# A hybrid attention layer on one core: projection pieces between the turns of attention of one k step in place of two

## The chip, the cores and the metric

One NeuronCore of a Trainium2 chip runs the whole layer in one launch. The metric is the device time of that launch in microseconds (us), as a median over runs. Five engines work side by side: TensorE (PE in the profile, with its weight loads as PEld), VectorE (DVE), ScalarE (ACT), GpSimd (POOL) and SyncE (SP), which here only issues DMAs.

## The reference: what is computed

One layer over 1024 positions of width 1024. The input is normalised and modulated by a condition, `u = LN(x) * (1 + scale) + shift`; one projection of `u` gives queries, keys, values and gates for 16 heads of 64 columns. Eight heads attend by softmax with a forget bias (FoX), eight by stick breaking. Each head's output is multiplied by `silu` of its gate branch, all are projected by `w_out`, and the gated residual is normalised again:

```python
u = (_layer_norm(x) * (1.0 + scale) + shift)
h = u @ w_in[layer]
fq, fk, fv, fg, ff, sq, sk, sv, sg = _split_columns(h)
# FoX:   s = q k^T * scale + (f_q - f_k), causal;  softmax(s) @ v
# stick: w = exp(log_sigmoid(z) + later), later = sum of log_sigmoid(-z) over later keys;  w @ v
y = jnp.concatenate([y_fox * silu(fg), y_sb * silu(sg)], axis=-1) @ w_out[layer]
x = _layer_norm(ALPHA * x + gate * y, ln_g, ln_b)
```

## The kernel before

Products keep float32 accuracy by splitting each operand in a high and a low part, so that one k step of a projection (128 of the 1024 input columns) is **three matmuls**: high by high, high by low, low by high. `u` stands transposed in SBUF as eight tiles `uh` and eight `ul`, one for each k step.

The heads go in eight pairs `p`; pairs 0 to 3 are stick breaking, 4 to 7 FoX. A **unit** `(p, h, i)` is one head of a pair and one block of 128 queries, and there are 128 units, counted `k` from 0. A unit takes two turns on TensorE:

- **scores turn** (`scores_turn`, L1060; `att_scores`, L447): the S matmuls (L459, L460) into the PSUM tile `S`, of which there is one (L71). Then ScalarE, VectorE and GpSimd make the weights from it. In pairs 0 to 3 ScalarE makes two sigmoids, `kp` (L481) and `be` (L483), VectorE runs the scan over `kp` (L488, L492), and GpSimd multiplies the two (L494). In pairs 4 to 7 VectorE adds the bias (L467), ScalarE exponentiates (L472), GpSimd scales (L475).
- **weights turn** (`weights_turn`, L1050; `att_transpose`, L499), two units later (`LAG`): the weights are transposed on TensorE, 128 columns at a time (L511, the tiles `T`), copied out by ScalarE (L513) and VectorE (L514), and for every second unit multiplied with the values (`att_pv`, L528).

Between these turns stands work of the next pairs, the **filler**: generators chained in one list (`fillers`, L997) that each do a piece and yield. `gen_m` (L321) makes a 128-column projection of queries, keys or gates: it fetches the weights (a DMA, then on GpSimd the high part, L126, and the low part, L127), yields, then runs two halves of 512 positions with eight k steps each (`m_step`, L296 to L298) and yields after every second step. `gen_v` and `v_tile` (L369, L348) make the values, 256 or 264 columns wide, for 128 positions at a time, with a yield in the middle and at the end; their weights come in four quarters, each read by two k steps. `gen_rest` finishes the projections of the start, `gen_last_g` (L983) the last gate, and loads the output weights as it goes. Three side tasks ride along, one call for each piece of their main chain (`beside`, L558): the adaLN gate, the forget bias and the splitting of `w_out`; their delays (`FLOG`, `FROW`, `GATE`, `SPACE`, L77 to L80) count pieces.

How many pieces a pair gets stands in `FILL` (L1007), 239 in all. The running sum `want` spreads them over two slots for each unit, nearly evenly, and `fill` (L1019) calls the chain until the count reaches the sum, so it rounds **up to whole pieces**. For the units of pairs 0 to 3 the loop (L1083) runs weights turn, scores turn, then both slots; from pair 4 on it runs scores turn, slot, weights turn, slot.

The order on TensorE is that in which the program is written. The other engines and SP's queue after the start are ordered by the scheduler of the framework. Weight buffers limit how early a fetch can run: two raw tiles (L115) and five high/low pairs in a ring (`RING`).

Of the kernel before, what the change touches and what calls it, by code (L numbers as in the profile page):

```python
# [27 lines left out]
def tile_hybrid_layer(  # L28
# [45 lines left out]
    RING = 5  # L74
    WARM = (4, 1, 1, 1, 1)
    NORM_ON = {6: nc.vector, 7: nc.vector}
    FLOG = 4  # L77
    FROW = 8
    GATE = 10
    SPACE = 5  # L80
    BEHIND = 1

    def after(*instructions):
# [226 lines left out]
    def make_g(p):  # L310
        sgt[p] = big("sg", 2, f"sg_{p}")
# [9 lines left out]
    def gen_m(p, m):  # L321
        tiles = fetch_m(p, m)
        yield
        (make_q, make_k, make_g)[m](p)
        for ch in ((1, 0) if m == 2 and p >= 4 else (0, 1)):
            acc = acc_tile(f"m_{p}_{m}_{ch}")
            for kt in range(NB):
                m_step(acc, tiles, kt, ch)
                if kt == NB - 1:
                    evac_m(p, m, ch, acc)  # L330
                if kt % 2 == 1:
                    yield


    fsb = cp.tile([P, 8, NB], F32, tag="fsb", name="fsb")
# [12 lines left out]
    def v_tile(g, t, acc, quarters):  # L348
        n = 264 if g == 1 else 256
        ts_ = slice(t * P, (t + 1) * P)  # L350
        for kt in range(NB):
            hi, lo = quarters[kt // 2]
            s = slice((kt % 2) * n, (kt % 2) * n + n)
            nc.tensor.matmul(acc[:, :n], u_hi[kt][:, ts_], hi[:, s], start=(kt == 0), stop=False)  # L354
            nc.tensor.matmul(acc[:, :n], u_lo[kt][:, ts_], hi[:, s], start=False, stop=False)  # L355
            nc.tensor.matmul(acc[:, :n], u_hi[kt][:, ts_], lo[:, s], start=False, stop=(kt == NB - 1))  # L356
            if kt == 3:
                yield
        for i in range(2):
            v4 = vt[2 * g + i].rearrange("p t (x c) -> p t x c", c=HD)  # L360
            a4 = acc[:, i * P:(i + 1) * P].rearrange("p (x c) -> p x c", c=HD)
            v_evacs.append(nc.scalar.copy(v4[:, t, 0::3, :], a4))
            v_evacs.append(nc.vector.tensor_tensor(v4[:, t, 1:3, :], a4, v4.bitcast(F32)[:, t, 0::3, :],
                                                   op=ALU.subtract))
        if g == 1:
            nc.vector.tensor_tensor(fsb[:, :, t], acc[:, 256:264], bf_sb, op=ALU.add)
        yield

    def gen_v(g, quarters=None, tiles=range(NB)):  # L369
        n = 264 if g == 1 else 256  # L370
        if quarters is None:
            quarters = []
            for h in range(4):
                src = w_vf[h] if g == 1 else w_v[g - (g > 1), h]
                quarters.append(fetch_w(f"v{g}_{h}", src, 2 * n))
        yield
        if g:
            make_v(g)
        for t in tiles:
            yield from v_tile(g, t, acc_tile(f"v_{g}_{t}"), quarters)  # L380

    def gen_forget():
# [23 lines left out]
        nc.tensor.matmul(fp, ones.to_broadcast([P, P]), pre, start=False, stop=True)  # L406
        fc = cp.tile([P, 64], F32, tag="fab", name="fc")
        nc.scalar.activation(fc, fp, AF.Copy, scale=-1.0)
        yield
        ft = t_tile("frow")[:64, :P]  # L410
        nc.tensor.transpose(ft, fc, ident)
# [349 lines left out]
    def gen_gate():  # L761
        b = att_tile("bg")
        nc.sync.dma_start(b, b_gate.to_broadcast([P, D]))
        for _ in range(GATE):
            yield
        parts = []
        for h in range(2):
            s = slice(h * 512, h * 512 + 512)
            hi, lo = (t[:, :512] for t in ring_w(f"gate_{h}"))
            nc.gpsimd.tensor_scalar(hi, gate[:, s], 1.0, 1.0, op0=ALU.mult, op1=ALU.mult)  # L770
            nc.gpsimd.tensor_tensor(lo, gate[:, s], hi.bitcast(F32), op=ALU.subtract)
            parts.append((hi, lo))
            for _ in range(2):
                yield
        for h in range(2):
            s = slice(h * 512, h * 512 + 512)
            gp = t_tile(f"gate_{h}")

            for i, part in enumerate(parts[h]):
                nc.tensor.matmul(gp, half.to_broadcast([P, P]), part, start=(i == 0), stop=(i == 1))  # L780
            nc.vector.scalar_tensor_tensor(gate[:, s], b[:, s], 0.5, gp, op0=ALU.mult, op1=ALU.add)
            yield

    def late_round(kb):
# [56 lines left out]
    def gen_rest():  # L841
        accs = {n: acc_tile(f"st_{n}b") for n in (3, 4)}
        order_of = {3: (3, 4, 5, 6, 7, 0, 1, 2), 4: range(NB)}
        for n in (3, 4):
            for j, kb in enumerate(order_of[n]):
                start_steps((n,), accs, kb, 512, 1024, ends=(j == 0, j == NB - 1))
                if j == NB - 1:
                    evac_m(*START[n], 1, accs[n])
                if j % 2:
                    yield  # L850

    bf_sb = cp.tile([P, 8], F32, tag="bf", name="bf_sb")
    nc.sync.dma_start(bf_sb, b_f.to_broadcast([P, 8]))
# [129 lines left out]
    def gen_last_g(p):  # L983
        tiles = fetch_m(p, 2)
        yield
        make_g(p)
        accs = {ch: acc_tile(f"m_{p}_2_{ch}") for ch in (1, 0)}
        for n in range(NB):
            for kt, ch in ([(0, 1 - n), (1, 1 - n)] if n < 2 else [(n, 1), (n, 0)]):
                m_step(accs[ch], tiles, kt, ch)  # L990
            if n == NB - 1:
                for ch in (1, 0):
                    evac_m(p, 2, ch, accs[ch])
            load_wo(n)
            yield

    fillers = chain([  # L997
# [6 lines left out]
                      gen_m(7, 0), gen_m(7, 1)]), gen_split_out()),  # L1004
        gen_last_g(7),
    ])
    FILL = (26, 36, 34, 34, 36, 36, 29, 8)  # L1007
    LEAD = 2
    LAG = 2
    W0 = 100.0  # L1010
# [35 lines left out]
    ready = []  # L1046
    LAST = 16 * (NPAIR - 1)
    tail = chain([gen_out_first(6), gen_out_last(6)] + [gen_out(t) for t in OUT_ORDER[1:]])
    fill(2)
    def weights_turn(k):  # L1050
        if LAG <= k < len(units) + LAG:
            u = units[k - LAG]
# [112 lines left out]
```

## Time and profile before

| | |
|---|---|
| median of 3 runs | 685.25 us (684.95, 685.25, 1349.6) |
| profiled execution, its own time | 685.27 us |
| its span, first to last instruction | 683.2 us |
| time around the span | 2.1 us |
| mean granted TensorE clock | 0.998 of full speed |

The span falls into a start (to about 81 us, where the projections of the first pair stand), the eight pairs of attention with the filler between their turns (81 to 564 us), and the rest of the last pair with the output projection. The busy time of TensorE has modelled ends: neighbouring matmuls overlap in it, so what a matmul costs is read from start to start in the timeline (a 128x512 matmul is listed with some 0.39 us, and the next starts 0.23 us behind it). `[0.38 <-POOL be L494]` behind a row of the timeline tells how long the engine had been idle and who ended it.

### The profile page before, as it was taken

The numbers are of one execution on the slowest core, as the hardware profiler recorded it, in microseconds if no ns is written. First come the engines' busy times: TensorE is split into PE (matmuls) and PEld (weight loads), VectorE is DVE, ScalarE is ACT, GpSimd is POOL, SyncE is SP. The second block draws the span as 40 slices with busy tenths as digits, with TensorE's granted clock in tenths as the row PEclk, the third lists the DMA queues.
The fourth block names the chain that finished last, engine by engine and source line by source line (L and its number), as shares of the span: only waits on it lengthen the run. The fifth ranks groups of instructions, "written<-read, shape, count | busy, mean of one in ns | idle before, by whom it ended". The sixth has DMA issues, their size and how long they took to land.

```text
span 683.2 us, 11185 instructions
## 1 busy us (share of the span) xinstructions
PE 670.8 (98%) x3713; PEld 571.9 (84%) x3713; DVE 485.1 (71%) x996; ACT 379.1 (55%) x857; POOL 404.6 (59%) x529
## 2 busy tenths in 40 slices
PE   8999999999999999999999999999999999999995
PEld 4788898888998888889988888889988888888885
DVE  6697779878666777786776675766676777875645
ACT  5567377756567666575665565655565666521000
POOL 5560179756357656566378878777785365655411
PEclk9999999999999999999999999999999999999999
DMA  9973422112102121122123455254352297143301
GB/s 330 410 274 141 140 74 79 29 39 59 32 15 65 45 64 42 40 54 55 49 92 129 166 161 169 79 173 147 117 163 73 61 356 300 59 178 104 119 32 61
DMA packets 45272, 81.54 MB, mean 119 GB/s; under 512 B 5216, under 2 KB 19360, under 8 KB 44960
## 3 DMA queue, kind: packets, MB, share of 16 engines
q1 hardware_dynamic: 43632, 76.54, 34.3%
q10 hardware_dynamic: 1584, 4.31, 1.9%
q8 instruction: 29, 0.48, 0.3%
q14 instruction: 27, 0.22, 0.1%
HBM read 60.34 MB, written 16.29 MB: 112 GB/s over the span
## 4 chain that ended last, share of the span: by engine, by line
PE 91%; DVE 2%; POOL 2%; ACT 2%; issue 1%; DMA 1%; SPq 0%; DVEq 0%; POOLq 0%; ACTq 0%
PE m L296 10%; PE m L298 10%; PE m L297 9%; PE pv L528 9%; PE T L511 9%; PE S L459 5%; PE S L460 5%; PE o L915 4%; PE o L913 4%; PE o L914 4%; PE v L356 4%; PE v L354 4%; PE v L355 4%; PE st_q L620 1%; PE st_late L620 1%
## 5 line engine op out<-in xcount | busy, mean ns | idle before, releaser
L514 DVE TENSOR_TENSOR pt<-T,pt 128x512 fp32r<-128x512 f32 (+2 forms) x192 | 102.8, 552 | 31.6 <-ACT pt L513 30.0
L296 PE MATMUL m<-uh,whi 128*128 128x512 f32 x304 | 122.8, 404 | 0.0
L513 ACT CAST pt<-T 128x512 fp32r<-128x512 f32 (+2 forms) x192 | 88.7, 478 | 58.9 <-PE T L511 54.9
L298 PE MATMUL m<-uh,wlo 128*128 128x512 f32 x304 | 119.7, 394 | 0.0
L297 PE MATMUL m<-ul,whi 128*128 128x512 f32 x304 | 119.6, 393 | 0.0
L494 POOL TENSOR_TENSOR be<-be,kp 128x127 f32<-128x127 f32 (+3 forms) x64 | 78.4, 1226 | 37.0 <-DVE kp L492 23.9
L488 DVE TENSOR_TENSOR_SCAN kp<-kp,floor 128x512 f32<-128x512 f32 (+2 forms) x64 | 65.0, 1015 | 26.3 <-ACT kp L481 25.1
L528 PE MATMUL pv<-pt,v 128*128 128x512 f32 x320 | 82.8, 389 | 0.0
L459 PE MATMUL S<-k,q 128*128 128x512 f32 (+5 forms) x192 | 69.4, 363 | 0.3 <-DVE nm L467 0.2
L475 POOL TENSOR_SCALAR a<-a,l 128x1024 f32<-128x1024 f32 (+3 forms) x64 | 48.1, 752 | 36.4 <-DVE l L473 26.8
L298 PEld LDWEIGHTS m<-uh,wlo 128*128 128x128 f32 x304 | 57.1, 188 | 13.7
L296 PEld LDWEIGHTS m<-uh,whi 128*128 128x128 f32 x304 | 57.1, 188 | 10.2
L460 PE MATMUL S<-kl,qz 128*128 128x512 f32 (+5 forms) x192 | 65.3, 341 | 0.0
L297 PEld LDWEIGHTS m<-ul,whi 128*128 128x128 f32 x304 | 57.2, 188 | 9.4
L472 ACT ACTIVATE a<-a,nm 128x1024 f32<-128x1024 f32 (+3 forms) x64 | 49.8, 778 | 26.7 <-DVE nm L467 26.1
L528 PEld LDWEIGHTS pv<-pt,v 128*128 128x128 f32 x320 | 55.5, 189 | 9.0
L544 POOL TENSOR_TENSOR ty<-ty,sg 64x256 f32<-64x256 f32 x64 | 47.0, 734 | 23.3 <-DVE ty L543 10.0
L467 DVE CUSTOM_DVE_ANT_0 a<-S,fb 128x1024 f32<-128x1024 f32 (+3 forms) x64 | 48.2, 753 | 16.2 <-PE S L460 12.0
L433 ACT CAST qz<-q 64x128 fp32r<-64x128 f32 x128 | 37.3, 296 | 34.1 <-PE S L460 32.8
L356 PE MATMUL v<-wlo_v,uh 128*128 128x256 f32 (+1 forms) x192 | 54.4, 283 | 0.8 <-POOL wlo_v L127 0.8
L354 PE MATMUL v<-whi_v,uh 128*128 128x256 f32 (+1 forms) x192 | 54.7, 285 | 0.0
L355 PE MATMUL v<-whi_v,ul 128*128 128x256 f32 (+1 forms) x192 | 54.1, 282 | 0.0
(290 smaller groups left out, 1609.8 us busy)
## 6 DMA issues: line engine op xcount, KB each, us to landing
raw<-in_w_qkg_dram SPq DMA_DIRECT2D x38, 256.0 KB, 2.7
wss<-in_w_ss_dram SPq DMA_DIRECT2D x12, 512.0 KB, 8.5
x<-in_x_dram SPq DMA_DIRECT2D x8, 512.0 KB, 7.3
k<-k SPq DMA_DIRECT2D x32, 128.0 KB, 2.3
wg<-in_w_gate_dram SPq DMA_DIRECT2D x8, 512.0 KB, 5.0
raw_o<-in_w_out_dram SPq DMA_DIRECT2D x16, 256.0 KB, 3.0
fb<-f_dr ACTq DMA_DIRECT2D x8, 512.0 KB, 4.3
wo_dr<-whi_o SPq DMA_DIRECT2D x16, 256.0 KB, 2.2
```

The costliest lines, as they stand in the source:

```text
L296: nc.tensor.matmul(acc, hi[:, c], u_hi[kt][:, s], start=(kt == 0), stop=False)
L297: nc.tensor.matmul(acc, hi[:, c], u_lo[kt][:, s], start=False, stop=False)
L298: nc.tensor.matmul(acc, lo[:, c], u_hi[kt][:, s], start=False, stop=(kt == NB - 1))
L354: nc.tensor.matmul(acc[:, :n], u_hi[kt][:, ts_], hi[:, s], start=(kt == 0), stop=False)
L355: nc.tensor.matmul(acc[:, :n], u_lo[kt][:, ts_], hi[:, s], start=False, stop=False)
L356: nc.tensor.matmul(acc[:, :n], u_hi[kt][:, ts_], lo[:, s], start=False, stop=(kt == NB - 1))
L459: nc.tensor.matmul(S[:, s, :w], qst[p][h][:, qs], kst[p][h][:, ks], start=True, stop=False)
L460: nc.tensor.matmul(S[:, s, :w], z, klo[p][:, ks], start=False, stop=True)
L494: nc.gpsimd.tensor_tensor(be[:, :ke - 1], be[:, :ke - 1], kp[:, 1:ke], op=ALU.mult)
L513: nc.scalar.copy(hi[:, :n, qo:qo + P], t3)
L514: lows[:] = [nc.vector.tensor_tensor(lo[:, :n, qo:qo + P], t3, hi.bitcast(F32)[:, :n, qo:qo + P], op=ALU.subtract)]
L528: nc.tensor.matmul(acc2[:, :, q0:], vt[p][:, kb, h * P:(h + 1) * P], pt[:, :, q0:], start=(kb == 0), stop=(kb == last))
```

## The change

A piece of filler becomes one k step (three matmuls) in place of two in `gen_m` and `gen_rest`, and two k steps of the narrower values in place of four in `v_tile`. All counts double: `FILL`, the four delays, the pieces called ahead of the loop, the delay in `gen_gate`, and the pieces in which nothing but a fetch is started, which become two. `gen_last_g` keeps its pieces of two steps and yields twice after each. The shares of a slot, `LEAD`, `LAG` and the work itself stay. The full diff:

```diff
--- before.py
+++ after.py
@@ -74,10 +74,10 @@
     RING = 5
     WARM = (4, 1, 1, 1, 1)
     NORM_ON = {6: nc.vector, 7: nc.vector}
-    FLOG = 4
-    FROW = 8
-    GATE = 10
-    SPACE = 5
+    FLOG = 8
+    FROW = 16
+    GATE = 20
+    SPACE = 10
     BEHIND = 1
 
     def after(*instructions):
@@ -321,6 +321,7 @@
     def gen_m(p, m):
         tiles = fetch_m(p, m)
         yield
+        yield
         (make_q, make_k, make_g)[m](p)
         for ch in ((1, 0) if m == 2 and p >= 4 else (0, 1)):
             acc = acc_tile(f"m_{p}_{m}_{ch}")
@@ -328,8 +329,7 @@
                 m_step(acc, tiles, kt, ch)
                 if kt == NB - 1:
                     evac_m(p, m, ch, acc)
-                if kt % 2 == 1:
-                    yield
+                yield
 
 
     fsb = cp.tile([P, 8, NB], F32, tag="fsb", name="fsb")
@@ -354,7 +354,7 @@
             nc.tensor.matmul(acc[:, :n], u_hi[kt][:, ts_], hi[:, s], start=(kt == 0), stop=False)
             nc.tensor.matmul(acc[:, :n], u_lo[kt][:, ts_], hi[:, s], start=False, stop=False)
             nc.tensor.matmul(acc[:, :n], u_hi[kt][:, ts_], lo[:, s], start=False, stop=(kt == NB - 1))
-            if kt == 3:
+            if kt in (1, 3, 5):
                 yield
         for i in range(2):
             v4 = vt[2 * g + i].rearrange("p t (x c) -> p t x c", c=HD)
@@ -373,6 +373,7 @@
             for h in range(4):
                 src = w_vf[h] if g == 1 else w_v[g - (g > 1), h]
                 quarters.append(fetch_w(f"v{g}_{h}", src, 2 * n))
+        yield
         yield
         if g:
             make_v(g)
@@ -406,6 +407,7 @@
         nc.tensor.matmul(fp, ones.to_broadcast([P, P]), pre, start=False, stop=True)
         fc = cp.tile([P, 64], F32, tag="fab", name="fc")
         nc.scalar.activation(fc, fp, AF.Copy, scale=-1.0)
+        yield
         yield
         ft = t_tile("frow")[:64, :P]
         nc.tensor.transpose(ft, fc, ident)
@@ -770,7 +772,7 @@
             nc.gpsimd.tensor_scalar(hi, gate[:, s], 1.0, 1.0, op0=ALU.mult, op1=ALU.mult)
             nc.gpsimd.tensor_tensor(lo, gate[:, s], hi.bitcast(F32), op=ALU.subtract)
             parts.append((hi, lo))
-            for _ in range(2):
+            for _ in range(4):
                 yield
         for h in range(2):
             s = slice(h * 512, h * 512 + 512)
@@ -779,6 +781,7 @@
             for i, part in enumerate(parts[h]):
                 nc.tensor.matmul(gp, half.to_broadcast([P, P]), part, start=(i == 0), stop=(i == 1))
             nc.vector.scalar_tensor_tensor(gate[:, s], b[:, s], 0.5, gp, op0=ALU.mult, op1=ALU.add)
+            yield
             yield
 
     def late_round(kb):
@@ -846,8 +849,7 @@
                 start_steps((n,), accs, kb, 512, 1024, ends=(j == 0, j == NB - 1))
                 if j == NB - 1:
                     evac_m(*START[n], 1, accs[n])
-                if j % 2:
-                    yield
+                yield
 
     bf_sb = cp.tile([P, 8], F32, tag="bf", name="bf_sb")
     nc.sync.dma_start(bf_sb, b_f.to_broadcast([P, 8]))
@@ -983,6 +985,7 @@
     def gen_last_g(p):
         tiles = fetch_m(p, 2)
         yield
+        yield
         make_g(p)
         accs = {ch: acc_tile(f"m_{p}_2_{ch}") for ch in (1, 0)}
         for n in range(NB):
@@ -993,6 +996,7 @@
                     evac_m(p, 2, ch, accs[ch])
             load_wo(n)
             yield
+            yield
 
     fillers = chain([
         beside(chain([gen_rest(), gen_v(0, v0_w, range(4, NB)), gen_m(1, 2)]), gen_gate()),
@@ -1004,7 +1008,7 @@
                       gen_m(7, 0), gen_m(7, 1)]), gen_split_out()),
         gen_last_g(7),
     ])
-    FILL = (26, 36, 34, 34, 36, 36, 29, 8)
+    FILL = (52, 72, 68, 68, 72, 72, 58, 16)
     LEAD = 2
     LAG = 2
     W0 = 100.0
@@ -1046,7 +1050,7 @@
     ready = []
     LAST = 16 * (NPAIR - 1)
     tail = chain([gen_out_first(6), gen_out_last(6)] + [gen_out(t) for t in OUT_ORDER[1:]])
-    fill(2)
+    fill(4)
     def weights_turn(k):
         if LAG <= k < len(units) + LAG:
             u = units[k - LAG]
```

With half pieces the sum is rounded up to a half where it was rounded up to a whole. Between two turns of attention there are 160 stretches of filler in pairs 0 to 6 (one for each unit up to pair 3, two from pair 4 on); by the written code 49 of them get half a piece more or less, and at any place the filler stands level with before or half a piece behind.

Three places in the built programs show it. The lines of the attention turns stand two higher in the changed program (L511 is L513, L528 is L530); those of the projections keep their numbers.

The first is TensorE in pair 0, about the weights turn of unit 14 (`T_1_6`: head 1, block 6); `m_0_0` is the query projection of pair 2, `uh_127` its fourth k step. Before:

```order
L296 MATMUL m_0_0_1550<-uh_127,whi_0_0_1512 128x512
L297 MATMUL m_0_0_1550<-ul_135,whi_0_0_1512 128x512
L298 MATMUL m_0_0_1550<-uh_127,wlo_0_0_1513 128x512
L511 MATMUL T_1_6_0_1564<-ident,be_1_6_1488 128x128 x4
L528 MATMUL pv_1_2_1571<-pt_1_2_0_1460,v_519 128x512 x4
L528 MATMUL pv_1_2_1571<-pt_1_2_1_1477,v_519 128x512
L528 MATMUL pv_1_2_1571<-pt_1_2_1_1477,v_519 128x2x128
L511 MATMUL T_1_6_1_1579<-ident,be_1_6_1488 128x128 x3
```

After:

```order
L513 MATMUL T_1_6_0_1561<-ident,be_1_6_1488 128x128 x4
L530 MATMUL pv_1_2_1568<-pt_1_2_0_1460,v_519 128x512 x4
L530 MATMUL pv_1_2_1568<-pt_1_2_1_1477,v_519 128x512
L530 MATMUL pv_1_2_1568<-pt_1_2_1_1477,v_519 128x2x128
L513 MATMUL T_1_6_1_1576<-ident,be_1_6_1488 128x128 x3
L461 MATMUL S_0_0_1582<-k_0_259,q_0_257 128x128
L462 MATMUL S_0_0_1582<-kl_261,qz_80 128x128
L296 MATMUL m_0_0_1550<-uh_127,whi_0_0_1512 128x512
```

Behind these rows the changed program goes on with the two score matmuls of unit 16 and then with the three matmuls of k step `uh_127` that stood ahead of the turn: the transposes come three 128x512 matmuls sooner.

The second is TensorE in pair 5, at the end of a key projection (`m_1_1`, its last k step `uh_131`) just ahead of the first value tile of pairs 6 and 7. Before:

```order
L296 MATMUL m_1_1_5195<-uh_131,whi_1_1_5072 128x512
L297 MATMUL m_1_1_5195<-ul_139,whi_1_1_5072 128x512
L298 MATMUL m_1_1_5195<-uh_131,wlo_1_1_5073 128x512
L511 MATMUL T_0_2_0_5270<-ident,a_0_2_5145 128x128 x3
L459 MATMUL S_1_7_5300<-k_1_4483,q_1_4274 128x512
```

After:

```order
L513 MATMUL T_0_2_0_5261<-ident,a_0_2_5145 128x128 x3
L296 MATMUL m_1_1_5195<-uh_131,whi_1_1_5072 128x512
L297 MATMUL m_1_1_5195<-ul_139,whi_1_1_5072 128x512
L298 MATMUL m_1_1_5195<-uh_131,wlo_1_1_5073 128x512
L461 MATMUL S_1_7_5300<-k_1_4483,q_1_4274 128x512
```

The last k step has gone behind the transposes of unit 85 (`T_0_2`). It reads `whi_1_1` and `wlo_1_1`, whose place in the ring the third value quarter (`whi_v_2`, `wlo_v_2`) takes next.

The third is GpSimd at that time: it splits weights of `w_out` (`o`) and the value quarters 0 to 3 (`v_0` to `v_3`), scales attention weights (`a`) and multiplies outputs by their gate (`ty`). TensorE's first value tile waits for `wlo_v_3`. Before:

```order
L475 TENSOR_SCALAR a_0_2_5145<-a_0_2_5145,l_0_2_5147 128x384
L127 TENSOR_TENSOR wlo_o_0_5206<-raw_o_0_5202,whi_o_0_5205 128x512
L127 TENSOR_TENSOR wlo_v_0_5279<-raw_v_0_5276,whi_v_0_5278 128x512
L475 TENSOR_SCALAR a_0_1_5186<-a_0_1_5186,l_0_1_5188 128x256
L126 TENSOR_SCALAR whi_v_1_5284<-raw_v_1_5282 128x512
L127 TENSOR_TENSOR wlo_v_1_5285<-raw_v_1_5282,whi_v_1_5284 128x512
L544 TENSOR_TENSOR ty_0_2_5226<-ty_0_2_5226,sg_4690 64x256
L126 TENSOR_SCALAR whi_v_2_5290<-raw_v_2_5288 128x512
L475 TENSOR_SCALAR a_0_0_5241<-a_0_0_5241,l_0_0_5243 128x128
L127 TENSOR_TENSOR wlo_v_2_5291<-raw_v_2_5288,whi_v_2_5290 128x512
L126 TENSOR_SCALAR whi_v_3_5296<-raw_v_3_5294 128x512
L127 TENSOR_TENSOR wlo_v_3_5297<-raw_v_3_5294,whi_v_3_5296 128x512
```

After (the low part `wlo_o_0` stands just ahead of the first of these rows):

```order
L546 TENSOR_TENSOR ty_0_3_5124<-ty_0_3_5124,sg_4690 64x256
L127 TENSOR_TENSOR wlo_v_0_5279<-raw_v_0_5276,whi_v_0_5278 128x512
L477 TENSOR_SCALAR a_0_2_5145<-a_0_2_5145,l_0_2_5147 128x384
L126 TENSOR_SCALAR whi_v_1_5284<-raw_v_1_5282 128x512
L127 TENSOR_TENSOR wlo_v_1_5285<-raw_v_1_5282,whi_v_1_5284 128x512
L477 TENSOR_SCALAR a_0_1_5186<-a_0_1_5186,l_0_1_5188 128x256
L126 TENSOR_SCALAR whi_v_2_5290<-raw_v_2_5288 128x512
L127 TENSOR_TENSOR wlo_v_2_5291<-raw_v_2_5288,whi_v_2_5290 128x512
L546 TENSOR_TENSOR ty_0_2_5226<-ty_0_2_5226,sg_4690 64x256
L126 TENSOR_SCALAR whi_v_3_5296<-raw_v_3_5294 128x512
L477 TENSOR_SCALAR a_0_0_5241<-a_0_0_5241,l_0_0_5243 128x128
L127 TENSOR_TENSOR wlo_v_3_5297<-raw_v_3_5294,whi_v_3_5296 128x512
```

The low part of `o_0` has moved ahead of `a_0_2` and `ty_0_3`, the third quarter ahead of `ty_0_2`, and the scaling of `a_0_0` now stands between the two parts of the fourth quarter.

## The prediction on record

> **What bounds the kernel now.** I read the page first: how busy TensorE is, at which clock, and in which slices.
>
> ```profile
> PE 670.8 (98%) x3713; PEld 571.9 (84%) x3713; DVE 485.1 (71%) x996; ACT 379.1 (55%) x857; POOL 404.6 (59%) x529
> PE   8999999999999999999999999999999999999995
> PEclk9999999999999999999999999999999999999999
> ```
>
> TensorE is busy nearly throughout at full clock; no other engine is near its limit. The change leaves the same products on TensorE and moves them, so it can win only what TensorE now waits, and lose only by new waits or dearer switches. The windows view, cut at the borders of the stages, tells how much waiting there is where filler stands (81 to 564 us): window, its length, TensorE's busy time first.
>
> ```profile
> 81.00:117.00 36.00, 35.55 (x225) 31.57 (x224) 26.87 (x48) 24.38 (x61) 28.86 (x41) 1.00 0.24 65
> 117.00:214.00 97.00, 96.87 (x587) 85.86 (x586) 72.94 (x129) 65.22 (x143) 58.57 (x76) 1.00 0.16 41
> 214.00:345.00 131.00, 130.96 (x761) 114.16 (x760) 97.98 (x162) 86.57 (x195) 75.47 (x107) 1.00 0.19 51
> 345.00:489.00 144.00, 143.07 (x824) 124.18 (x824) 95.37 (x249) 80.49 (x200) 111.75 (x125) 1.00 0.43 136
> 489.00:564.00 75.00, 74.78 (x385) 62.26 (x385) 53.94 (x140) 46.27 (x112) 44.75 (x54) 1.00 0.50 164
> ```
>
> Idle are 0.45, 0.13, 0.04, 0.93 and 0.22 us, together **1.77 us** of 483. The rest of the span is the start and the end, whose order on TensorE the change leaves as it is. The waits of TensorE by name, those that fall in these windows:
>
> ```profile
> PE v L356 <- POOL wlo_v L127: 0.8, 1, 0.8
> PE T L511 <- POOL be L494: 0.4, 1, 0.4
> PE S L459 <- DVE nm L467: 0.2, 1, 0.2
> ```
>
> Three waits make 1.4 of the 1.77 us. So the whole change plays for less than 0.3% of the time, unless it makes switching between filler and attention dearer.
>
> **Term 1, the price of a switch.** The timeline of TensorE shows three kinds of border in one place: a filler run that starts behind transposes, two pieces in a row, and one that starts behind scores.
>
> ```profile
> 407.78 0.71 PE L511 MATMUL T<-ident,a 128*128 128x128 f32 x5
> 408.24 0.48 PE L296 MATMUL m<-uh,whi 128*128 128x512 f32 x1
> 408.56 0.40 PE L297 MATMUL m<-ul,whi 128*128 128x512 f32 x1
> 408.80 0.39 PE L298 MATMUL m<-uh,wlo 128*128 128x512 f32 x1
> 409.03 0.40 PE L296 MATMUL m<-uh,whi 128*128 128x512 f32 x1
> 409.26 0.39 PE L297 MATMUL m<-ul,whi 128*128 128x512 f32 x1
> ...
> 409.84 0.28 PE L460 MATMUL S<-kl,qz 128*128 128x256 f32 x1
> 409.95 0.40 PE L296 MATMUL m<-uh,whi 128*128 128x512 f32 x1
> 410.19 0.40 PE L297 MATMUL m<-ul,whi 128*128 128x512 f32 x1
> ```
>
> Behind the 128-column transposes the first 128x512 matmul holds the next one off for 0.32 us (408.24 to 408.56); behind another step it is 0.23 (409.03 to 409.26), behind scores of 256 columns 0.24. So a border between two k steps is free, and what costs 0.09 us is a wide matmul behind a 128-column one. Such transposes are followed by something wide anyway, scores if not filler. In TensorE's order there are 185 places where a matmul over 128 columns follows one of 128, and 186 in the changed program: six turns that led to scores now lead to a projection, and the one more stands behind the transpose of the forget row. That is 1 x 0.09 = **+0.1 us**; bounds 0 and, if each of the ten filler runs more (160 for 150) paid it, 0.9.
>
> The Trainium skill speaks against cutting finer: "TensorE: Matmul & The Clock Gate", section LDWEIGHTS (loading the stationary operand), puts a load of 128 weight columns at P / 1.2 ns, 107 ns, more than a 128-column matmul streams, so that a load behind such a matmul isn't covered. The trace agrees in kind, with 0.09 us behind transposes and none behind wider scores. By the rule's whole 0.107 us, taken for each of the ten runs more, the term would be an estimated 1.1 us in place of 0.1, and the time 686.2.
>
> **Term 2, the transposes that come sooner.** Where filler moves from before a weights turn to behind it, the transposes start three matmuls, 3 x 0.23 = 0.70 us, sooner after their scores, and the other engines have that much less time for the weights. I compared for the 128 units when GpSimd ends the weights and when the transposes start. From unit 16 on the margin is 0.8 to 10 us, more than the 0.70. Only in pair 0 is it short, and of its units the change brings 0, 9, 14 and 15 forward (unit 0 has over 5 us). Timelines of GpSimd, then TensorE, for units 9, 14 and 15:
>
> ```profile
> 114.27 1.55 POOL L494 TENSOR_TENSOR be<-be,kp 128x767 f32<-128x767 f32 x1
> 134.93 1.78 POOL L494 TENSOR_TENSOR be<-be,kp 128x895 f32<-128x895 f32 x1
> 139.54 2.00 POOL L494 TENSOR_TENSOR be<-be,kp 128x1023 f32<-128x1023 f32 x1 [2.08 <-DVE kp L492]
> ```
>
> ```profile
> 111.56 0.66 PE L511 MATMUL T<-ident,be 128*128 128x128 f32 x4 [0.38 <-POOL be L494]
> 116.58 0.82 PE L511 MATMUL T<-ident,be 128*128 128x128 f32 x6
> 137.22 0.60 PE L511 MATMUL T<-ident,be 128*128 128x128 f32 x4
> 142.28 0.49 PE L511 MATMUL T<-ident,be 128*128 128x128 f32 x3
> ```
>
> The margins are 116.58 - 115.82 = 0.76, 137.22 - 136.71 = 0.51 and 142.28 - 141.54 = 0.74 us. Less 0.70 that leaves 0.06, -0.19 and 0.04: one new wait of 0.19 us, at unit 14. Unit 8 (111.56) has its wait of 0.38 already; its stretch keeps its filler, so the wait stays. Term: **+0.2 us**. Bounds: 0 if the weights come sooner too, 3 x 0.70 = 2.1 if they come 0.7 us later than now. I take the margins as they stand, since the work ahead of these weights is the same.
>
> **Term 3, the wait for the value weights.** TensorE, then GpSimd, at the first value tile of pairs 6 and 7:
>
> ```profile
> 452.17 0.39 PE L298 MATMUL m<-uh,wlo 128*128 128x512 f32 x1
> 456.95 0.28 PE L355 MATMUL v<-whi_v,ul 128*128 128x256 f32 x1
> 458.05 0.39 PE L356 MATMUL v<-wlo_v,uh 128*128 128x256 f32 x1 [0.82 <-POOL wlo_v L127]
> ```
>
> ```profile
> 444.35 1.29 POOL L127 TENSOR_TENSOR wlo_o<-raw_o,whi_o 128x512 fp32r<-128x512 f32 x1
> 451.27 1.30 POOL L127 TENSOR_TENSOR wlo_v<-raw_v,whi_v 128x512 fp32r<-128x512 f32 x1
> 452.53 0.72 POOL L544 TENSOR_TENSOR ty<-ty,sg 64x256 f32<-64x256 f32 x1
> 453.23 0.61 POOL L126 TENSOR_SCALAR whi_v<-raw_v 128x512 fp32r<-128x512 f32 x1
> 453.83 0.36 POOL L475 TENSOR_SCALAR a<-a,l 128x128 f32<-128x128 f32 x1
> 454.17 1.28 POOL L127 TENSOR_TENSOR wlo_v<-raw_v,whi_v 128x512 fp32r<-128x512 f32 x1
> 456.02 0.62 POOL L126 TENSOR_SCALAR whi_v<-raw_v 128x512 fp32r<-128x512 f32 x1 [0.57 <-DMA raw_v<-in_w_v_dram]
> 456.72 1.27 POOL L127 TENSOR_TENSOR wlo_v<-raw_v,whi_v 128x512 fp32r<-128x512 f32 x1
> ```
>
> From start to start TensorE loses 458.05 - 456.95 less 0.12 for the matmul, 0.98 us. The fourth quarter is late because its DMA waits for a raw tile, and that in a chain for the low part at 444.35. The changed order puts that low part ahead of a scaling and a gate product, about 1.3 us sooner, so the DMA no longer decides. The ring does: the third quarter needs the place that the key projection's last step reads, and that step now ends behind the transposes, about 0.25 us after 452.56, at 452.8. From there GpSimd's new order has the high and low part of quarter 2 (0.68, then 1.27), the gate product (0.70), the high part of quarter 3 (0.60), the scaling (0.34) and its low part (1.27): 457.7. Now the low part ends at 457.99, so **-0.3 us**. Bounds: -0.98 if the wait goes, +0.4 if the scaling that now stands between the two parts comes on top of a chain that is no shorter.
>
> **What costs nothing.** The four delays doubled keep their place to half a piece; the gate's two matmuls for each half stand up to a half piece sooner and nothing near waits for them. Projections end up to 0.7 us later; their results are for the next pair and have a whole pair, over 30 us, to cover that. SP issues the same DMAs; where two swapped, a weight tile's landing (the page's list of DMA issues, last number) is covered by the pieces of the tiles fetched before it:
>
> ```profile
> raw<-in_w_qkg_dram SPq DMA_DIRECT2D x38, 256.0 KB, 2.7
> ```
>
> If that cover is gone, it shows as a wait like that of term 3, up to 1 us.
>
> **Sum**, on the profiled execution's own 685.27 us, which is the median of the runs shown to 0.02: +0.1 + 0.2 - 0.3 = 0.0, so 685.3 us.
>
> **The rivals.** *A, evener slots close the waits:* all 1.77 us in the windows go, 683.5 us. For it speaks that 0.93 of it is one wait whose order did change; against it that the stretches about units 8 and 10 get no more filler. 13%. *B, slower: TensorE outruns GpSimd in pair 0.* Place: units 9, 14 and 15. From the point where their weights come 0.06 us later than now each costs what it is late, up to 0.70 us: 685.3 + 2.1 - 0.2 + 0.3 for a third term that fails = 687.5 us. For it speaks that GpSimd also splits weights there, in 1.3 us blocks that the scheduler puts in between; against it the 55 to 61% load of that engine. 16%. *C, each new border is a switch:* 239 borders at 0.09 us would be 21.5 us, 706.8 us. The trace shows none at a border between steps. 1%. *D, the change doesn't do what it says:* 111 of 160 stretches keep their share, and the scheduler hides the others, 685.3 us with nothing moved: 15%.
>
> **How the numbers follow.** My forecast, 685.3 us, has 55%. Its own bounds come from those of the terms: -0.1 - 0.2 - 0.7 below and, with term 2 left to B, +0.8 + 0.7 above, 684.3 to 686.8. The range is widened below towards A and above to half way into B: **683.9 to 687.1**. All cases but C lie within 2%, which is about what a measurement of this kernel can tell from no change: faster by more 1%, within 97%, slower by more 2%.
>
> **What would show it.** Right: the five windows' idle time still 1 to 2.5 us together; the wait for `wlo_v` at the value tile of pair 5 shorter, 0.5 to 0.7 us; a new wait of about 0.2 us at unit 14's transposes, and that of unit 8 unchanged; border to border 0.23 us between steps. Wrong: a wait over 0.5 us on `be` in pair 0 (B), no wait left there and at the values (A), or filler steps over 0.3 us apart at borders (C). A wait of another name in pairs 1 to 6 would be one that I have not seen.

## The result and the profile after

| | before | after |
|---|---|---|
| median | 685.24 us | 683.79 us |
| lowest and highest (without the one of 1349.6) | 684.42, 686.2 | 683.47, 684.15 |
| profiled execution, its own time | 685.27 us | 684.15 us |
| its span | 683.2 us | 682.4 us |
| ratio after to before | | 0.998 (95% interval 0.9974 to 0.9986) |

The changed kernel is **1.45 us faster**, 0.2%. I had said 685.3 us and a range from 683.9 us; it lies just below that. The profiled execution of after is the slowest of its runs, so the two profiled times differ by 1.12 us, not by 1.45.

Of the windows between unit 0 and the end of the filler, the first three columns matter: window, its length, TensorE's busy time.

```profile
81.00:117.00 36.00, 35.96 (x228) 32.15 (x227) 27.48 (x49) 24.30 (x62) 29.45 (x42) 1.00 0.25 65
117.00:214.00 97.00, 96.69 (x582) 84.92 (x580) 72.26 (x128) 64.77 (x142) 58.14 (x74) 1.00 0.16 41
214.00:345.00 131.00, 130.50 (x754) 113.64 (x755) 97.20 (x163) 86.52 (x194) 74.53 (x106) 1.00 0.19 51
345.00:489.00 144.00, 144.00 (x833) 125.67 (x833) 95.91 (x250) 83.14 (x202) 112.87 (x126) 1.00 0.44 138
489.00:564.00 75.00, 74.96 (x387) 62.47 (x386) 54.92 (x141) 46.34 (x111) 44.90 (x55) 1.00 0.50 164
```

Idle are now 0.04, 0.31, 0.50, 0.00 and 0.04 us, 0.89 together, where there were 1.77. But it isn't the old waits made smaller. Most of the old ones have gone, and others have come or grown elsewhere. TensorE's waits by name, those in these windows:

```profile
PE T L513 <- POOL wlo L127: 0.3, 1, 0.3
PE S L461 <- ACT be L485: 0.3, 1, 0.3
```

From start to start of TensorE's rows, less what the same matmul takes elsewhere, the places stand so (us lost in the two profiled executions):

| place | before | after |
|---|---|---|
| transposes of unit 7 | 0.22 | 0.00 |
| transposes of unit 8 | 0.53 | 0.20 |
| product with the values behind them | 0.00 | 0.15 |
| transposes of unit 14 | 0.00 | 0.30 |
| transposes of unit 31, scores of unit 33 | 0.26 | 0.93 |
| transposes of unit 82 | 0.28 | 0.00 |
| first value tile of pairs 6 and 7 | 0.97 | 0.00 |
| scores of unit 106 | 0.37 | 0.00 |
| filler at 548 us | 0.21 | 0.34 |
| together | 2.84 | 1.92 |

That is -0.92 us. Counted from the first scores (81.09 us before, 81.42 after) to the end, the traces differ by 1.11 us, so the table holds most of it. The 0.33 us by which the first scores come later in after arise in the start, ahead of all that moves; in the other traces the first scores lie anywhere from 80.79 to 81.50 us.

Another part is in no trace. The time around the span is 2.05 us (median) in before and 1.73 in after, 0.32 less. The 1.45 us between the medians are about these 0.32 and the 1.11. No run here shows what makes the time around the span shorter.

**The value weights.** GpSimd in after, the low parts of `o_0` and of the second, third and fourth quarter (`v_1` to `v_3`); then TensorE, the key projection's last k step and two products of the first value tile that read the fourth quarter:

```profile
442.54 1.31 POOL L127 TENSOR_TENSOR wlo_o<-raw_o,whi_o 128x512 fp32r<-128x512 f32 x1
447.94 1.30 POOL L127 TENSOR_TENSOR wlo_v<-raw_v,whi_v 128x512 fp32r<-128x512 f32 x1
450.52 1.29 POOL L127 TENSOR_TENSOR wlo_v<-raw_v,whi_v 128x512 fp32r<-128x512 f32 x1
453.41 1.29 POOL L127 TENSOR_TENSOR wlo_v<-raw_v,whi_v 128x512 fp32r<-128x512 f32 x1
```

```profile
452.68 0.48 PE L296 MATMUL m<-uh,whi 128*128 128x512 f32 x1
...
456.97 0.28 PE L355 MATMUL v<-whi_v,ul 128*128 128x256 f32 x1
457.09 0.28 PE L356 MATMUL v<-wlo_v,uh 128*128 128x256 f32 x1
```

The last low part ends at 454.70 us, where it ended at 457.99 and I expected 457.7. SP's queue shows how the fetches got there, before and then after (the x2 at 447.74 are issues at 447.74 and 452.60 us):

```profile
446.05 0.54 SPq L873 DMA_DIRECT2D wo_dr<-wlo_o  x1
446.64 0.43 SPq L122 DMA_DIRECT2D raw_v<-in_w_v_dram  x1
447.17 0.48 SPq L283 DMA_DIRECT2D k<-k  x1
447.74 5.18 SPq L122 DMA_DIRECT2D raw_v<-in_w_v_dram  x2
```

```profile
443.87 0.32 SPq L875 DMA_DIRECT2D wo_dr<-wlo_o  x1
444.24 0.43 SPq L122 DMA_DIRECT2D raw_v<-in_w_v_dram  x1
...
445.82 0.33 SPq L122 DMA_DIRECT2D raw_v<-in_w_v_dram  x1
446.24 1.87 SPq L283 DMA_DIRECT2D k<-k  x2
449.27 0.33 SPq L122 DMA_DIRECT2D raw_v<-in_w_v_dram  x1
```

The second quarter's fetch stands in SP's queue behind the store of `o_0`'s low part, and of the two raw tiles it takes the one that this low part frees, so both wait for the same row of GpSimd. That row ends 1.79 us sooner (443.85 for 445.64), and the fetch follows it after 0.39 us in place of 1.00, together 2.40 us (444.24 for 446.64). The fetch is also shorter, from issue to landing, before and then after:

```profile
DMA to landing us min/median/max: 3.9/3.9/3.9
```

```profile
DMA to landing us min/median/max: 2.9/2.9/2.9
```

The third quarter's fetch now stands ahead of the key rows (445.82 for 447.74). All that follows on GpSimd moves with these fetches.

**The new waits.** TensorE about unit 31, before and after, then ScalarE after:

```profile
213.87 0.40 PE L298 MATMUL m<-uh,wlo 128*128 128x512 f32 x1
214.10 1.04 PE L511 MATMUL T<-ident,be 128*128 128x128 f32 x8
215.18 0.38 PE L459 MATMUL S<-k,q 128*128 128x256 f32 x1
```

```profile
213.56 0.40 PE L298 MATMUL m<-uh,wlo 128*128 128x512 f32 x1
214.25 1.07 PE L513 MATMUL T<-ident,be 128*128 128x128 f32 x8 [0.30 <-POOL wlo L127]
215.57 0.39 PE L461 MATMUL S<-k,q 128*128 128x256 f32 x1 [0.25 <-ACT be L485]
```

```profile
208.14 1.28 ACT L388 ACT_TABLE_LOAD   x1
211.35 1.28 ACT L389 ACT_TABLE_LOAD   x1
212.81 0.95 ACT L515 CAST pt<-T 128x512 fp32r<-128x512 f32 x2
213.78 1.28 ACT L483 ACT_TABLE_LOAD   x1
215.25 0.27 ACT L485 ACTIVATE be<-S 128x128 f32<-128x128 f32 x1
```

Here the forget bias's side task takes ScalarE to other functions and back, three table loads of 1.28 us. From the scores of unit 31 to those of unit 33 the stretch takes 11.32 us before and 11.33 after: ScalarE sets it, for the scores of unit 33 start 0.05 us behind its last row in both. (Its own pace hangs on VectorE too: behind the first load it waits 1.65 us for the side task's `fab`, 1.66 in before.) The transposes' 0.30 us are named after `wlo`, which they don't read. Their weights had ended on GpSimd 1.3 us earlier; what they lacked, by the semaphores that they wait for, was a tile `T`, and VectorE had copied that out only at 214.10, behind ScalarE's late copy:

```profile
213.41 0.69 DVE L516 TENSOR_TENSOR pt<-T,pt 128x512 fp32r<-128x512 f32 x1 [2.37 <-ACT pt L515]
```

Before has 30 filler matmuls in the stretch, after 27. The three that left it follow behind, where the next two units take 7.57 us in place of 6.85. This stretch, which another engine sets, had room for that filler at no cost, and the half piece moved out of it costs its whole **0.7 us**.

At unit 14 the wait that I forecast is there: the transposes start 0.54 us behind the last filler matmul, 0.23 without a wait, when the weights have ended on GpSimd at 134.88 + 1.77 = 136.65 us.

```profile
134.88 1.77 POOL L496 TENSOR_TENSOR be<-be,kp 128x895 f32<-128x895 f32 x1
```

```profile
136.24 0.40 PE L298 MATMUL m<-uh,wlo 128*128 128x512 f32 x1
136.78 0.41 PE L513 MATMUL T<-ident,be 128*128 128x128 f32 x2
```

### The profile page after: what moved, and what is told of

It is laid out like the page before. It is cut to its first block, busy times and chain, and to the rows that moved or that the text cites. A ratio compares the mean times of both kernels' runs of the same rounds, so it can differ in the third digit from the quotient of the medians.

```text
span 682.4 us, 11191 instructions
## 1 busy us (share of the span) xinstructions
PE 671.7 (98%) x3713; PEld 572.5 (84%) x3713; DVE 485.0 (71%) x996; ACT 380.7 (56%) x857; POOL 404.9 (59%) x529
## 4 chain that ended last, share of the span: by engine, by line
PE 95%; ACT 2%; DVE 2%; POOL 1%; issue 0%; DVEq 0%; POOLq 0%
PE m L296 10%; PE m L297 10%; PE m L298 10%; PE pv L530 10%; PE T L513 9%; PE S L462 5%; PE S L461 5%; PE o L917 4%; PE o L916 4%; PE o L915 4%; PE v L354 4%; PE v L356 4%; PE v L355 4%; PE st_q L622 1%; PE st_late L622 1%; PE st_k L622 1%
## 5 line engine op out<-in xcount | busy, mean ns | idle before, releaser
L530 PE MATMUL pv<-pt,v 128*128 128x512 f32 x320 | 82.9, 389 | 0.0
L530 PEld LDWEIGHTS pv<-pt,v 128*128 128x128 f32 x320 | 55.5, 189 | 9.0
L483 ACT ACTIVATE kp<-S 128x128 f32<-128x128 f32 (+3 forms) x64 | 42.0, 657 | 21.8 <-PE S L462 20.5
```

What stands on the lines that cost most here:

```text
L530: nc.tensor.matmul(acc2[:, :, q0:], vt[p][:, kb, h * P:(h + 1) * P], pt[:, :, q0:], start=(kb == 0), stop=(kb == last))
```

## The experiments

Most of them put half pieces in a part of the program only. They are the changed program with the running sum rounded up to whole old pieces wherever a condition on the unit `k` doesn't hold:

```diff
-    def fill(want):
+    def fill(want, k=-1):
+        if not (CONDITION):
+            want = 2 * -int(-want // 2)
         while done[0] < want:
...
-            fill(want[2 * k + LEAD + 1])
+            fill(want[2 * k + LEAD + 1], k)
...
-        fill(want[2 * k + LEAD + 2])
+        fill(want[2 * k + LEAD + 2], k)
```

All times in us; "before" is the kernel before on the same chip.

| run | condition or edit | median (lowest, highest) | before | ratio, 95% interval |
|---|---|---|---|---|
| e1 | none: whole pieces | 685.68 (684.28, 686.26) | 685.23 | 1.0001 (0.9992, 1.001) |
| e2 | 80 to 87 | 683.14 (682.75, 684.56) | 685.23 | 0.9974 (0.9964, 0.9984) |
| e3 | 0 to 15 | 684.87 (684.45, 685.92) | 685.23 | 0.9995 (0.9987, 1.0004) |
| e4 | 16 to 63 | 684.85 (684.57, 686.12) | 685.23 | 0.9992 (0.998, 1.0003) |
| e5 | 64 to 95 | 683.36 (682.85, 684.09) | 685.47 | 0.9972 (0.9962, 0.9983) |
| e6 | from 96 | 684.15 (683.76, 684.94) | 685.47 | 0.9983 (0.9974, 0.9991) |
| e7 | bias load at unit 110 | 686.96 (686.09, 688.82) | 685.47 | 1.0024 (1.0013, 1.0034) |
| e8 | all but 24 to 35 | 683.24 (683.02, 683.53) | 685.47 | 0.9969 (0.9957, 0.998) |
| e9 | 80 to 83 | 683.15 (682.79, 683.49) | 685.15 | 0.9972 (0.996, 0.9983) |
| e10 | 84 to 87 | 684.62 (684.12, 685.7) | 685.15 | 0.9993 (0.9984, 1.0002) |
| e11 | 80 to 87 and from 96 | **682.60** (682.58, 682.99) | 685.15 | 0.9965 (0.9952, 0.9977) |
| e12 | output weights later | 685.17 (684.74, 686.39) | 685.15 | 0.9999 (0.999, 1.0008) |
| e13 | bias load at unit 107 | 685.00 (684.42, 685.44) | 685.46 | 0.9991 (0.9982, 1.0) |
| e14 | e9 and e13 together | 683.15 (682.91, 683.45) | 685.46 | 0.996 (0.9947, 0.9972) |

### Where the gain lies: e1 to e6

The conditions are, in this order:

```diff
+        if not (False):
+        if not (80 <= k < 88):
+        if not (0 <= k < 16):
+        if not (16 <= k < 64):
+        if not (64 <= k < 96):
+        if not (96 <= k):
```

**e1.** 

> The changed program, with every slot's sum rounded up to an even count, so that filler comes in pieces of two k steps everywhere again. Both theories: the order is that of before but for a few rows of the side tasks, so 685.2 us (684.9 to 685.5), with the wait for wlo_v of about 0.8 us in pair 5 back. If it were 684.5 or less, the gain would lie in the yields of the side tasks and not in the half pieces.

The wait for `wlo_v` was back, but the median says little here: the times fell in two groups, five from 684.28 to 684.92 and six from 685.68 to 686.26. Two things follow. The lower group lies some 0.6 us under before's usual times, though the pieces are whole. TensorE's rows at unit 8 show where some of it is from:

```profile
110.65 0.39 PE L298 MATMUL m<-uh,wlo 128*128 128x512 f32 x1
111.15 0.66 PE L513 MATMUL T<-ident,be 128*128 128x128 f32 x4
```

The transposes come 0.50 us behind the last filler (0.27 lost; 0.53 in before), and unit 7's wait is gone. In pair 0 nothing differs from before on TensorE but the place of the adaLN gate's four matmuls, two k steps of the values sooner. The gate's parts lie in the ring of weight buffers (`ring_w`), and the high part of a projection's weights on GpSimd, which waits for these matmuls, goes ahead of the weights of unit 6, into time in which GpSimd was idle. In before and then in e1:

```profile
104.01 0.62 POOL L126 TENSOR_SCALAR whi<-raw 128x512 fp32r<-128x512 f32 x1
```

```profile
102.41 0.62 POOL L126 TENSOR_SCALAR whi<-raw 128x512 fp32r<-128x512 f32 x1 [1.87 <-PE gate L782]
```

The weights of units 7 and 8 end 0.6 us sooner, counted from the first scores. At unit 8's transposes e1 has gained 0.59 us, but 0.15 of it is lost again at the product behind them, which leaves 0.44. The changed program's 0.66 (0.52 behind the product) comes another way: its GpSimd has the high part behind unit 6's weights as before, and the scores of unit 6 come a half piece, 0.71 us, sooner.

The upper group is in the profile, since the profiled execution is of it. TensorE, then VectorE, then the load of the last head's bias (issued at 547.7 us, landing 7.1 us later):

```profile
557.45 0.50 PE L461 MATMUL S<-k,q 128*128 128x512 f32 x1 [1.13 <-DVE nm L469]
```

```profile
554.86 0.29 DVE L447 TENSOR_TENSOR fb<-fb,causal_ps 128x128 f32<-128x128 f32 x1 [1.49 <-DMA fb<-f_dr]
```

```profile
L422 ACTq DMA_DIRECT2D fb<-f_dr x1: 327/327/327, 547.7 to 547.7; - x1
...
DMA to landing us min/median/max: 7.1/7.1/7.1
```

VectorE waits for the bias, and behind it stands the row that frees the score tile. In before's profiled execution the same load took 5.5 us and nothing waited.

**e2.** 

> Half pieces only in the slots of units 80 to 87 (first half of pair 5), whole ones elsewhere. Theory V (the gain is the one wait for the value weights in pair 5, whose size my third term had too small): the wait goes wholly, and with the wait of 0.26 at unit 82 the kernel takes 684.0 to 684.3, nearly all of the 1.45 us. Theory E (rival: evener slots close many short waits, each worth 0.2 to 0.5 us): no more than 0.5 us of the gain lies here, 684.7 to 685.2.

It gained more than either theory gave, 2.1 us: units 80 to 87 alone do at least as well as the whole change. The trace shows what was left out: 1.26 us at the two waits (unit 82 and the value weights), 0.44 at unit 8 by the gate's move as in e1, and a time around the span that is 0.21 us shorter (1.84 for 2.05).

**e3.** 

> Half pieces only in the slots of units 0 to 15 (pair 0). Theory V: this region gives and takes alike (waits at units 7 and 8 close, 0.22 and 0.33 us; new ones at units 9 and 14, 0.2 and 0.3), 685.1 to 685.3. Theory E: the closed waits show in the time, 684.6 to 684.9. My prediction on record has here a loss of 0.2 (unit 14), 685.4.

**e4.** 

> Half pieces only in the slots of units 16 to 63 (pairs 1 to 3). Here the changed program has the waits at units 31 to 33 that before does not have, some 0.75 us together, and closes none. Both theories: slower than before by that, 685.7 to 686.0. If it is 685.2, these waits are luck of one execution and not of the order.

Both intervals hold 1, so pair 0 and pairs 1 to 3 neither win nor lose measurably against before. e4 did have the waits at units 31 to 33 in its profile (0.29 and 0.25 us idle); against them stand e1's 0.44 us from the gate and a time around the span that is 0.31 us shorter. My expectation of a loss had left both out. In e3 that time is 0.28 us shorter.

**e5.** 

> Half pieces only in the slots of units 64 to 95 (pairs 4 and 5). Theory V (the value weights of pair 5 alone, now seen to be worth 2.1 us with units 80 to 87): as with units 80 to 87 alone, 683.0 to 683.3. Theory E (waits in many places): other than that by 0.5 us or more, either way.

As e2: the rest of pairs 4 and 5 adds nothing.

**e6.** 

> Half pieces only in the slots from unit 96 on (pairs 6 and 7). A third theory, F, came from the kernel with whole pieces: in its profiled execution the scores at 557.45 us waited 1.13 us for VectorE, which had waited 1.49 us for the load of the last head's forget bias fb (7.1 us from issue to landing, 5.5 in before, 4.8 in the changed program), and its times fall in two groups, 684.3 to 684.9 and 685.7 to 686.3. F says that half pieces in pair 6 reorder the loads that stand beside this one, so that it lands in time: no execution above 685.3, median 684.5 to 684.8. Theory V, with the value weights as the only cause: 685.2, with both groups.

1.3 us faster, though the wait for `wlo_v` is still there (0.5 us idle). It has no upper group, and the scores of unit 106 no longer wait. There VectorE, in before and then in after, frees the score tile of unit 105:

```profile
526.53 0.69 DVE L271 SCALAR_TENSOR_TENSOR q<-m,q 64x512 fp32r<-64x512 f32 x1 [0.39 <-ACT q L270]
527.24 1.09 DVE L467 CUSTOM_DVE_ANT_0 a<-S,fb 128x896 f32<-128x896 f32 x1
```

```profile
525.76 1.09 DVE L469 CUSTOM_DVE_ANT_0 a<-S,fb 128x896 f32<-128x896 f32 x1 [0.54 <-PE S L462]
527.21 0.68 DVE L271 SCALAR_TENSOR_TENSOR q<-m,q 64x512 fp32r<-64x512 f32 x1
```

The query projection's result stood ahead of the bias in VectorE's order; with half pieces the projection ends later and its row stands behind. Each part's gain (0.4, 0.4, 2.1 and 1.3 us) holds the gate's 0.44 us and 0.2 to 0.3 us around the span, so they don't add up to the whole change.

### The value weights apart: e9 and e10

```diff
+        if not (80 <= k < 84):
+        if not (84 <= k < 88):
```

**e9.** 

> Half pieces only in the slots of units 80 to 83. GpSimd and SP get the changed order about the value weights (the low part of o_0 ahead of ty and a, the third quarter's fetch ahead of the key rows), while the key projection's last k step stays ahead of the transposes of unit 85. Theory O (the order of GpSimd and SP is the whole of the value-weight gain): the wait for wlo_v is gone, 683.1 to 683.5 as with units 80 to 87. My prediction's working (the ring place that the last k step frees decides what is left): the wait goes here too, and would come back in part only with the step moved. If the wait stays, the moved k step was the cause.

**e10.** 

> Half pieces only in the slots of units 84 to 87. On TensorE just three matmuls move, the last k step of the key projection goes behind the transposes of unit 85; GpSimd's order is that of whole pieces. Theory O: the wait for wlo_v stays at 0.9 to 1.0 us, 685.0 to 685.7 with both groups of times. If the moved step is what closes the wait, 683.1 to 683.9.

Theory O holds on both sides. e9 has no wait for `wlo_v` and takes 683.15, as e2. In e10 on TensorE only the last k step has moved, GpSimd's order is e1's, and the wait stands:

```profile
457.75 0.38 PE L356 MATMUL v<-wlo_v,uh 128*128 128x256 f32 x1 [0.85 <-POOL wlo_v L127]
```

So the k step behind the transposes, on which I had put the rest of the wait, takes no part, and what e9 shares with e2 about the value weights is the order of GpSimd and SP. (e9 reaches it by two half pieces that move on TensorE at 420 and 427 us; no run changes that order alone.) The wait at unit 82 went with e9 as well (0.28 us); no run parts it from the value weights.

### The new waits: e8

```diff
+        if not (not 24 <= k < 36):
```

> The changed program with whole pieces back in the slots of units 24 to 35 alone, where it had got new waits (units 31 to 33, 0.75 us together). If these are real in every execution, it takes 683.0 to 683.2, faster than the changed program's 683.8 by 0.6 to 0.8. If not, 683.8.

683.24, 0.55 us below the changed program's median (0.75 by the two ratios to before), with 30 filler matmuls again between the scores of units 31 and 33. That agrees with the 0.67 us of the traces.

### The two groups: e7, e12, e13, e14

```diff
-            if 4 <= p < NPAIR - 1 and i == 0:
+            if 4 <= p < NPAIR - 1 and i == (1 if k == 110 else 0) and k != 111:
```

**e7.** 

> The kernel before with one edit: the forget bias of the last head is loaded behind the scores of unit 110 in place of 111, some 4 us sooner. Pieces are the old ones. Theory F: the upper group of times goes, none above 685.3, median 684.5 to 684.9, and the scores near 556 us wait for nothing. If the spread of before (684.4 to 686.2) and its median 685.2 stay, F is wrong and the loads are no cause.

Slower than before by 1.5 us. The bias was in time, but the key rows' load had lost its place in SP's queue to another (issued at 549.61 us, 548.27 in before), and the scores waited for it. The profiled execution is the fastest of e7's, so this wait is not all of the 1.5 us, and the rest is not shown:

```profile
PE S L459 <- DMA k<-k: 0.5, 1, 0.5
```

```diff
-            load_wo(n)
+            for pr in {0: (), 1: (), 7: (5, 6, 7)}.get(n, (n - 2,)):
+                load_wo(pr)
```

**e12.** 

> The kernel before, with the loads of the output weights in pair 6 (512 KB each) started two steps of the gate projection later, the last three pairs' together in the last step, so that fewer loads stand beside that of the last head's bias fb. Theory F (the upper group of before's times comes from the load of fb landing late beside other loads): fb lands within 5 us, none above 685.3 from this cause, median 684.5 to 684.9; a new wait for the output weights at the end of pair 7 would cost and would show by its name. If the spread stays as it was, the load's neighbours are not the cause.

The same as before: the bias took 6.4 us, and VectorE waited for it (0.6 us). Moving the loads of output weights away didn't help.

```diff
-            if 4 <= p < NPAIR - 1 and i == 0:
+            if 4 <= p < NPAIR - 1 and (k == 107 or (i == 0 and k != 111)):
```

**e13.** 

> The kernel before with the load of the last head's forget bias fb behind the scores of unit 107 in place of 111; no other row moves on any engine. Theory F (the upper group comes from this load landing late): no wait of VectorE for fb, the scores near 556 us wait for nothing, no execution above 685.3, median 684.7 to 685.0. If the upper group (685.7 to 686.5) stays, F is wrong.

**e14.** 

> Half pieces in the slots of units 80 to 83 and the load of fb behind unit 107. By theory F the value-weight gain and the fb gain add: 682.8 to 683.2 with a spread under 0.5 us; e9 without the load's move has 682.8 to 683.5, median 683.15, so the gain here is at most 0.3.

In e13 the upper group is gone: none above 685.44, where before had 5 of 15 from 685.9 up. The median fell by 0.46 us, at the edge of what these runs tell, and 0.14 of it lies around the span (1.94 for 2.08). The load itself, issued at 532.3 us:

```profile
DMA to landing us min/median/max: 3.5/3.5/3.5
```

So theory F is supported: e1's trace shows an execution of the upper group waiting for the load, and with the load moved that group isn't seen. Eleven executions are few, though. Over all sessions 25 of before's 111 executions (without the one of 1349.6) lie from 685.85 up; at that rate none in eleven comes by chance about once in 17 times. What makes it land after 4.8 to 7.1 us at its old place, and why the half pieces in pair 6 bring it in sooner (4.8 in the changed program, 5.2 in e6), is open. e14 gains nothing over e9, whose VectorE waited 0.2 us for the load.

The Trainium skill, "DMA: Bandwidth & Descriptors", section Issuing engines are not separate DMA queues, says that transfers that ScalarE, SP or GpSimd start run on the same 16 DMA engines and interleave. The 3.5 us at the new place, where without this load these engines are busy 6% of the time (531 to 536 us), and the 4.8 to 7.1 at the old one, where they are busy 77% in before (545 to 553 us), agree with it. It isn't the whole of it: the changed program's engines are busy 93% there, and its load landed after 4.8 us, the soonest.

### The version that beats both: e11

```diff
+        if not (80 <= k < 88 or k >= 96):
```

> Half pieces in the slots of units 80 to 87 and from unit 96 on, whole ones elsewhere: the two places that gave a gain by themselves, without those that got new waits. By the waits seen in the profiles: 683.1 of units 80 to 87, less 0.3 for the scores wait of unit 106 that half pieces in pair 6 close, and without executions of the upper group: 682.6 to 683.0, faster than the changed program (683.8). If half pieces help by being even and not by their place, it is slower than the changed program.

682.60 us, 2.55 below before and 1.2 below the changed program's median; the intervals of the two ratios to before (0.9952 to 0.9977, 0.9974 to 0.9986) barely meet. Half pieces aren't better by being half: the larger gains in these traces lie where another engine's order changed with them.

## Why the prediction was wrong, point by point

- **What bounds the kernel: right within the span.** The idle time of TensorE in the five windows went from 1.77 to 0.89 us. Outside it 0.32 us went (2.05 to 1.73), a part that the prediction took as fixed; without it the result would have lain just inside the range.
- **Term 1, switches (+0.1): right in size.** What a wide matmul loses behind a 128-column one sums to 15.5 us over 185 places before and to 15.4 over 186 after. By the estimate drawn from the Trainium skill, "TensorE: Matmul & The Clock Gate", section LDWEIGHTS (loading the stationary operand), ten runs more should have cost 1.1 us. The trace shows nothing of it, though the profile of before lists the weight loads of the projections with 188 ns each, more than the 107 of that estimate.
- **Term 2, transposes that come sooner (+0.2): right at unit 14 (0.30 us), wrong in what it left out.** I compared the transposes with the weights on GpSimd alone and wrote that from unit 16 on the margin is enough. At units 31 to 33 it is ScalarE that decides, with the table loads of a side task in its order, and that cost 0.67 us more than before.
- **Of unit 8, "its stretch keeps its filler, so the wait stays": the step that failed in pair 0.** Of its wait 0.33 us went (0.15 came back at the product behind it), and all of unit 7's 0.22. What failed behind it is "I take the margins as they stand, since the work ahead of these weights is the same": where filler moves behind a scores turn, the scores and with them GpSimd's work come sooner too, 0.71 us at unit 6. Of the gate's matmuls, "nothing near waits for them" failed as well: in e1, which has whole pieces, a row of GpSimd waits for just these.
- **Term 3, the wait for the value weights (-0.3): the mechanism's direction right, its size wrong, -0.97.** The wait went wholly, which was the term's own lower bound. The failed step is "The ring does: the third quarter needs the place that the key projection's last step reads". In the changed program that quarter's low part is written at 450.52 us, the fourth's high part at 452.48, and the step starts at 452.68, so neither takes that place; the words on the ring in the section on the change are wrong too. With no such hold the fetches decide: the low part of `o_0` 1.79 us sooner, the fetch behind it 0.61 us closer and 1.0 us shorter, and the fourth quarter's low part ends 3.29 us sooner, not 0.3.
- **Waits of another name:** I gave the waits at units 82 and 106 no term. They were in the trace (0.28 and 0.37 us), and half pieces closed both.
- **The sum.** In the traces the waits that had a term give +0.30 and -0.97, and those that had none give -0.40 (units 7 and 8), -0.65 (82 and 106), +0.67 (31 to 33) and +0.13 (548 us), together only -0.25. It is luck that they nearly cancel.
- **The rivals.** A came nearest in number, 683.5 us, but not in mechanism: 0.89 us of idle time are left, 0.32 of the gain lie around the span, and it isn't evenness that closes the waits, for e2, uneven nearly everywhere, does at least as well as the change. B (687.5) didn't happen, though the "55 to 61% load" that I held against it isn't that of pair 0: GpSimd is busy 28.86 of 36 us in the first window, 80%. C (706.8) and D (nothing moved) didn't happen either; C's switches are counted above.
- **Not in the prediction at all:** before's own spread. Three of its 21 executions in the result's table end at 685.86 us or above, by a late load as far as e1 and e13 show; none of the changed program's 22 does. On the median this tells little.

## What to carry to other kernels

When filler moves, a margin has to be taken against every engine that the turn waits for, ScalarE's copies and side tasks too, and not only against the one that usually ends last. It has to be taken anew, too, since the scores, and the work that hangs on them, move with the filler. Where a scheduler orders the other engines, the larger effects of such a change can come from the orders that shift with it, as here: read GpSimd's, VectorE's and SP's order at each wait, and follow each fetch back to the row that frees its buffer and to what stands ahead of it in the queue. A finer grain is worth trying place by place: two places here gave 2.55 us, the whole change 1.45.

## What the runs showed of the hardware

- A load of 512 KB took 3.5 us from issue to landing at 532 us (e13) and 4.8 to 7.1 us at 545 to 548 us in the other programs. In e1, whose load took 7.1 us in the profiled execution, the times fell in two groups with medians of 684.45 and 686.05 us.
- Taking ScalarE to other functions and back took three table loads of 1.28 us each (208.14, 211.35 and 213.78 us above). The copy ahead of the last one ended 0.02 us before it, so nothing else stands there between a row and a load.
- Time around the profiled span differs between kernels (2.05 us before, 1.73 after, 1.96 in e7) and stays within 0.13 us over the runs of one (1.67 to 1.80 in after); spans alone would have shown 0.3 us too little of the gain. What makes the difference is open.
